# Retention's values and SSD's dt in one pass at the head of the mixers, and S5's products summed on VectorE

## The chip, the cores and the metric

The kernel runs on one core of one Trainium2 chip. The metric is the device time of one execution in microseconds, as the median of several runs; lower is better. The engines are named as the profile names them: PE is TensorE (PEld is its weight load), DVE is VectorE, ACT is ScalarE, POOL is GpSimd, SP is SyncE, which issues all DMA transfers in order.

## What is computed

Two trunk layers of a hybrid backbone run over 640 tokens: a prompt of 128 and a sample of 512, each with its own modulation. All matrices are float32. Cut to what matters:

```python
h = rmsnorm(x, norm1_w) * (1.0 + sc1) + sh1
proj = h @ w_in                                   # 1024 x 2568, split into the four mixers' columns
pa, pb, pc, pd = jnp.split(proj, [o1, o2, o3], axis=-1)
# ssd_mixer:       z, xbc, dt = split(pa);  dt = softplus(dt + dt_bias)  (8 columns: 2 directions x 4 heads)
# retention_mixer: q, k, v, g = split(pb);  y_f, y_b = chunked_decay_scan(q, k, v, ...); silu(g) * groupnorm(y)
# s5_mixer:        bbar = coef * b (complex);  bu = u bbar;  diagonal scan;  y = Re(x c);  GLU
# lru_mixer:       conv, gates, diagonal scan, gelu gate
y = jnp.concatenate([ya, yb, yc, yd], axis=-1) @ w_out
x = x + g1 * y
h = rmsnorm(x, norm2_w) * (1.0 + sc2) + sh2
x = x + g2 * conv_ffn(h, w_up, conv_w, conv_b, w_down)
```

The values are the 256 columns of `v` of the retention mixer, and dt is 8 columns of the SSD mixer.

## The kernel before

Activations stand channels by tokens, as 8 tiles of 128 channels and 640 tokens, in two halves of 320 tokens (`HALF`). A float32 product is made of three float32r matmuls: weight and activation are each split into a rounded part (`hi`) and a remainder (`lo`), and hi*hi, lo*hi and hi*lo are added in PSUM (`mm3`, line 209).

A **column tile** (`col_tile`, 214) is 128 output columns of a weight: 8 k-tiles by 3 matmuls by 2 halves, 48 matmuls of 320 columns. Its weights come through `wsplit` (186): per 512 columns a DMA of 256 KB into a `raw` tile, a cast on ACT into `hi`, a subtraction into `lo`. There are 5 raw tiles (`RAWS`) and 5 pairs of `hi` and `lo` (`SPLITS`), so a tile takes 2 of 5 pairs until its last matmul.

The mixers of a layer are Python generators (`s5_mixer` 820, `lru_mixer` 973, `gates` 1050 for `gb` and `z`, `ssd_mixer` 1110, `ret_mixer` 1277). `layer` (1399) steps them in the order of the string `ORDER` (45). A planner then orders each engine's instructions by a simulated time, with the program's order as priority. Two rules bind it: tiles of one tag in PSUM (`bank`, 139: three `mm`, two `b`, one each of `a`, `c` and `mod`) get their first write in the order of the program (lines 96 to 101), and each engine's queue, SP's too, is worked off in order.

What stands around the change:

- **Layer front.** The half of tokens 320 to 639 is normed first (`HO`). In layer 1 `first_tiles` (232), called at the first step of `s5_mixer`, runs the three first tiles (two of S5, one of LRU) over that half in the banks `mm`, and then over the other half in steps of two k-tiles in `mm`, `a`, `c` and `b`, as the norm delivers them. In layer 0 the norm itself comes in four steps, and `first_tiles` follows them.
- **S5's preparation** (`s5_prep`, 590). For four groups q it makes the products of the input matrix with powers of the state matrix, transposes them into PSUM (`c`), copies them (`wbs`), stores them to DRAM (`wb`) and loads them back for the scans. In layer 1 the complex product is finished on VectorE (`cmul`) and transposed. In layer 0 VectorE makes four real products alone, and the sums are made on PE: `T.matmul` with the identity, two products added in PSUM, and again in the product with `cm`.
- **dt** (1110 to 1137). The 8 columns are the stationary operand, `hi` and `lo` side by side as 16, and `hh` streams: 2 halves by 8 k-tiles by 2 parts, 32 matmuls of 320 columns, then a copy, five transposes and two additions.
- **Values** (1340 to 1359). They stand token-major: the activation is stationary and the weights stream. Five chunks of 128 tokens by 8 k-tiles by 3 matmuls of 256 columns, 120 in all, go to the banks `b`, two chunks in a bank, so their first write comes after that of S5's GLU tiles, which are in `b` too. The four pairs of `hi` and `lo` are all needed until the last chunk. Then comes `attend(0)`.

Of the kernel before, what the change touches and what calls it, by code (L numbers as in the profile page):

```python
# [9 lines left out]
F32 = mybir.dt.float32  # L10
# [33 lines left out]

ORDER = ("s5 gb lru lru gb ssd ssd z lru ssd z ret ret ssd ret ssd ret ret ret ret",
         "s5 ssd gb lru ssd lru gb z lru ssd z ret ssd ret ret ssd ret ret ret ret")
RAWS = 5
# [28 lines left out]
def hybrid_kernel(ctx: ExitStack, tc: tile.TileContext, I, O, dbg=None):  # L76
# [67 lines left out]
    def r2f(ap):  # L144
        return ap.bitcast(F32)
# [40 lines left out]
    def wsplit(ap, n, cut=512, le=None, tag=None):  # L186

        out = []
        for c0 in range(0, n, cut):
            w = min(cut, n - c0)  # L190
            raw = wp.tile([P, 512], F32, tag="raw", name="raw", bufs=RAWS)
            SP.dma_start(raw[:, :w], ap[:, c0:c0 + w])
            if tag:
                hi, lo = page(tag, F32R, "whi")[:, :512], page(tag, F32R, "wlo")[:, :512]
            else:
                hi = wp.tile([P, 512], F32R, tag="hi", name="hi", bufs=SPLITS)
                lo = wp.tile([P, 512], F32R, tag="lo", name="lo", bufs=SPLITS)
# [392 lines left out]
    def s5_prep(l):  # L590
# [94 lines left out]
        for q in range(2):  # L685
# [14 lines left out]
            for h in range(2):  # L700
# [29 lines left out]
             [bb[:, i] for i in range(2)], [bt[:, i] for i in range(2)])  # L730
        if l == 0:
            nbb = paged(p2, [16, 16], "nbb")
            V.tensor_scalar(nbb, bb[:, 1], -1.0, None, op0=M_)
        ncq = paged(p2, [16, 16], "ncq")
# [10 lines left out]
        for q in range(4):  # L745
# [8 lines left out]
            def big(tag):  # L754
                return paged(p3, [4, 8, 16], tag)

            pm, tt = [big("pmr"), big("pmi")], [big("pt1"), big("pt2")]
            if l:
                cmul([wide(bb[:, i]) for i in range(2)], [pwr(v) for v in ap], pm, tt)
                parts = [[v] for v in pm]  # L760

                yield
            else:

                for t, b, a in ((pm[0], bb[:, 0], ap[0]), (tt[0], nbb, ap[1]), (pm[1], bb[:, 1], ap[0]),
                                (tt[1], bb[:, 0], ap[1])):
                    V.tensor_tensor(t, wide(b), pwr(a), op=M_)
                parts = [[pm[0], tt[0]], [pm[1], tt[1]]]
            parts = [[v.rearrange("p k a b -> p k (a b)") for v in vs] for vs in parts]
# [13 lines left out]
            for i in range(2):  # L783
                for j, v in enumerate(parts[i]):
                    for k in range(4):
                        T.matmul(ps[32 * k:32 * k + 32, 0:128], cm[i][:, o + k, :], v[:, k], start=i + j == 0,
                                 stop=i == 1 and j == len(parts[i]) - 1, tile_position=(0, 32 * k))
            kt = paged(p3, [128], "kt")
# [321 lines left out]
    def ssd_mixer(l, hh, y):  # L1110

        dr = smp.tile([P, 8, 8], F32, tag="dtraw", name="dtraw")
        SP.dma_start(dr, I["w_dt"][l].rearrange("p (k c) -> p k c", c=8))
        dw = smp.tile([P, 8, 16], F32R, tag="dtw", name="dtw")
        V.tensor_copy(dw[:, :, 0:8], dr)
        V.tensor_tensor(dw[:, :, 8:16], dr, r2f(dw[:, :, 0:8]), op=S_)
        yield
        if TSC:
            V.tensor_scalar(pr(l, "scw", 0, 20), pr(l, "scw", 0, 20), 0.5, None, op0=M_)
        dtc = page("C", name="dtc")  # L1120
        old = sec[0]
        sec[0] = old + "*"
# [6 lines left out]
        sec[0] = old  # L1129
        ps = bank("c")  # L1130
        for t in range(5):
            T.transpose(ps[:, 16 * t:16 * t + 16], dtc[0:16, 128 * t:128 * t + 128], idn[0:16, 0:16])
        raw = sm([5, 8])
        pv = ps[:, :80].rearrange("p (a b) -> p a b", b=16)
        V.tensor_tensor(raw, pv[:, :, 0:8], pr(l, "dtb").unsqueeze(1).to_broadcast([P, 5, 8]), op=A_)
        V.tensor_tensor(raw, raw, pv[:, :, 8:16], op=A_)
        dt = smp.tile([P, 40], F32, tag="dt", name="dt")
# [137 lines left out]


    def ret_mixer(l, hh, y):
        swap = [(i + 16) % 32 for i in range(32)]
# [60 lines left out]
        yield  # L1339
        units = wsplit(I["w_in"][l, 14], 1024) + wsplit(I["w_in"][l, 15], 1024)  # L1340
        vk = [paged("B", [5, 128], "rv") for _ in range(2)]
        for c0 in (0, 2, 4):
            n = min(2, 5 - c0)
            ps = bank("b")
            old = sec[0]
            sec[0] = old + "*"
            for c in range(n):
                for k in range(8):
                    hi, lo = units[k // 2][2:]
                    w = slice((k % 2) * 256, (k % 2) * 256 + 256)  # L1350

                    mh, ml = [v[:, 128 * (c0 + c):128 * (c0 + c) + 128] for v in hh[k]]
                    o = ps[:, 256 * c:256 * c + 256]
                    T.matmul(o, mh, hi[:, w], start=k == 0, stop=False)
                    T.matmul(o, mh, lo[:, w], start=False, stop=False)
                    T.matmul(o, ml, hi[:, w], start=False, stop=k == 7)
            sec[0] = old
            for i in range(2):
                A.copy(vk[i][:, c0:c0 + n], ps[:, 0:256 * n].rearrange("p (c w) -> p c w", w=256)[:, :, 128 * i:128 * i + 128])
        attend(0, q, kx)  # L1360
# [38 lines left out]
    def layer(l, norm):  # L1399
# [4 lines left out]
        for ks in steps or (range(8),):  # L1404
            if l == 0 and ks[0]:
                mod_first(ks[0] // 2)
            for h in HO:
# [5 lines left out]
                "ret": ret_mixer(l, hh, ys["ret"]), "gb": gates(l, hh, (2, 3), ys["lru"], AF.Gelu_apprx_tanh),  # L1413
                "z": gates(l, hh, (9, 11), ys["ssd"], None if TSZ else AF.Silu)}
        for n in gens:
# [11 lines left out]
        for i, n in enumerate(order):  # L1427
# [364 lines left out]
```

## Time and profile before

| what | value |
|---|---|
| median of 3 runs | 1727.2 us (1725.74 to 1730.68) |
| the profiled execution's own time | 1727.16 us |
| its span, first to last instruction | 1725.4 us |
| PE busy, mean granted clock | 1655.2 us (96%), 0.982 |
| DVE, ACT, POOL busy | 1027.9, 713.1, 230.5 us |
| moved by DMA | 205.99 MB |

The profiled execution is some 1.8 us longer than its span and agrees with the median. Layer 0's mixers lie at about 60 to 390 us of the span, layer 1's at about 928 to 1212 us; the feed-forward parts lie behind each. A busy PE is not a PE at its peak: matmuls overlap, one of 320 columns is shown for 0.31 us, and the next begins 0.15 us after it. All instructions have line 92, the helper that records them, so groups are told apart by their tiles.

### The profile page before, as it was taken

How to read it: one execution, taken by the hardware profiler on the slowest of the kernel's cores; microseconds unless marked ns; L12 is line 12 of the kernel's file. 1: busy time of each engine (PE TensorE's matmuls, PEld its weight loads, DVE VectorE, ACT ScalarE, POOL GpSimd, SP SyncE). 2: the span in 40 equal slices, each digit the busy share in tenths (PEclk: the TensorE clock that was granted, in tenths of full speed). 3: DMA queues.
4: the chain of work that ended last, by engine and by line, in shares of the span. 5: the costliest groups of instructions: out<-in, count | busy, mean ns of one | idle time of the engine just before them, and what ended most of it. 6: DMA issues, size and time to landing. Idle time of an engine off the chain costs nothing.

```text
span 1725.4 us, 31021 instructions
## 1 busy us (share of the span) xinstructions
PE 1655.2 (96%) x11630; PEld 1540.3 (89%) x11630; DVE 1027.9 (60%) x2566; ACT 713.1 (41%) x1567; POOL 230.5 (13%) x445
## 2 busy tenths in 40 slices
PE   7887999999999999999999999999899999999997
PEld 3766887888999999999998998888899999999996
DVE  7776876878783454364357797677754333333346
ACT  5734526645441432232245653663452232232244
POOL 0000001000222111211220010100021211111221
PEclk9989999999999999999999999989999999999999
DMA  9565564321346545554232344422122222322321
GB/s 337 159 186 156 175 190 147 92 77 62 123 143 195 172 151 159 174 173 115 86 117 92 104 134 134 138 66 77 38 68 62 86 75 61 92 74 57 91 74 61
DMA packets 143433, 205.99 MB, mean 119 GB/s; under 512 B 24900, under 2 KB 64692, under 8 KB 143284
## 3 DMA queue, kind: packets, MB, share of 16 engines
q1 hardware_dynamic: 143284, 204.02, 37.7%
q8 instruction: 92, 1.51, 0.4%
q14 instruction: 57, 0.47, 0.1%
HBM read 183.89 MB, written 20.07 MB: 118 GB/s over the span
## 4 chain that ended last, share of the span: by engine, by line
PE 82%; DVE 6%; DMA 3%; ACT 2%; issue 1%; SPq 1%; POOL 0%; DVEq 0%; ACTq 0%
PE mm L92 67%; PE b L92 7%; PE c L92 3%; PE mod L92 3%; PE a L92 2%; DVE x L92 1%; SPq L92 1%; DVE lo L92 1%; DVE nt L92 1%; DMA mraw<-in_mod_w 1%; DMA wb<-wb 0%; DMA scb<-cumd 0%; DVE s5r L92 0%; DVE nsq L92 0%; DVE nacc L92 0%
## 5 line engine op out<-in xcount | busy, mean ns | idle before, releaser
L92 PE MATMUL mm<-hhi,hi 128*128 128x320 f32 x1880 | 594.8, 317 | 7.9 <-ACT hhi L92 5.8
L92 PE MATMUL mm<-hhi,lo 128*128 128x320 f32 x1880 | 590.4, 314 | 3.1 <-DVE lo L92 3.1
L92 PE MATMUL mm<-hlo,hi 128*128 128x320 f32 x1880 | 589.6, 315 | 0.8 <-DVE hlo L92 0.8
L92 ACT CAST hi<-raw 128x512 fp32r<-128x512 f32 (+1 forms) x378 | 223.5, 593 | 512.2 <-PE mm L92 290.6
L92 PEld LDWEIGHTS mm<-hhi,hi 128*128 128x128 f32 x1880 | 357.5, 190 | 25.1 <-issue 7.6
L92 PEld LDWEIGHTS mm<-hhi,lo 128*128 128x128 f32 x1880 | 357.1, 190 | 7.7 <-DVE lo L92 4.6
L92 PEld LDWEIGHTS mm<-hlo,hi 128*128 128x128 f32 x1880 | 356.8, 190 | 6.8 <-DVE hlo L92 1.8
L92 POOL TENSOR_TENSOR lo<-raw,hi 128x512 fp32r<-128x512 f32 (+1 forms) x134 | 166.5, 1243 | 531.0 <-ACT hi L92 324.2
L92 DVE SCALAR_TENSOR_TENSOR x<-mm,mod,x 128x128 f32<-128x128 f32 (+2 forms) x284 | 114.3, 433 | 184.8 <-PE mm L92 183.5
L92 PE MATMUL mm<-fah,lo 128*128 128x320 f32 x640 | 197.4, 309 | 0.0
L92 PE MATMUL mm<-fah,hi 128*128 128x320 f32 x640 | 196.4, 311 | 0.4 <-DVE x L92 0.4
L92 PE MATMUL mm<-fal,hi 128*128 128x320 f32 x640 | 195.9, 309 | 0.0
L92 DVE TENSOR_TENSOR lo<-raw,hi 128x512 fp32r<-128x512 f32 (+1 forms) x244 | 162.7, 668 | 43.9 <-ACT hi L92 39.0
L92 DVE TENSOR_SCALAR fc<-fraw,par 128x643 f32<-128x643 f32 x44 | 27.5, 625 | 189.7 <-ACT fraw L92 189.5
L92 PEld LDWEIGHTS mm<-fah,hi 128*128 128x128 f32 x640 | 119.5, 188 | 4.9 <-issue 1.6
L92 PEld LDWEIGHTS mm<-fah,lo 128*128 128x128 f32 x640 | 120.3, 188 | 0.4 <-issue 0.4
L92 PEld LDWEIGHTS mm<-fal,hi 128*128 128x128 f32 x640 | 119.8, 188 | 0.0
L92 DVE TENSOR_TENSOR fa<-fc,mm 128x320 f32<-128x320 f32 (+1 forms) x128 | 44.1, 374 | 102.8 <-PE mm L92 100.4
L92 DVE SCALAR_TENSOR_TENSOR fc<-fraw,par,fc 128x643 f32<-128x643 f32 x88 | 85.0, 967 | 1.7
L92 ACT COPY fraw<-mm 128x320 f32<-128x320 f32 (+2 forms) x124 | 38.3, 344 | 85.4 <-PE mm L92 82.0
L92 PE MATMUL mod<-mraw,s 128*32 128x256 f32 x768 | 63.5, 395 | 7.7 <-DMA mraw<-in_mod_w 6.8
L92 POOL MEMSET fraw<- 128x2 f32 x132 | 7.4, 101 | 395.4 <-DVE nrs L92 211.5
(395 smaller groups left out, 2518.3 us busy)
## 6 DMA issues: line engine op xcount, KB each, us to landing
raw<-in_up SPq DMA_DIRECT2D x176, 256.0 KB
mraw<-in_mod_w SPq DMA_DIRECT2D x160, 256.0 KB
raw<-in_w_in SPq DMA_DIRECT2D x80, 256.0 KB
raw<-in_dn SPq DMA_DIRECT2D x96, 192.0 KB
mraw<-in_mod SPq DMA_DIRECT2D x32, 256.0 KB
raw<-in_w_o SPq DMA_DIRECT2D x32, 256.0 KB
tb<-tb SPq DMA_DIRECT2D x16, 326.0 KB
x<-in_x SPq DMA_DIRECT2D x16, 320.0 KB
```

Source lines behind the costliest of these rows:

```text
L92: r = f(*a, **k)
```

## The change

A new generator `values` makes the values and dt in one pass. It is first in `ORDER` in both layers. The 8 dt columns of two k-tiles are split into the same tiles as the 256 value columns, so that a k-tile is 264 columns wide, and `SPLITS` tiles grow from 512 to 528 columns. Each chunk of 128 tokens has a bank `mm` of its own and 24 matmuls of 264 columns. dt now comes out token-major and has its bias added straight from PSUM; the 32 matmuls, the copies, the five transposes and the addition of the two parts go away. `ret_mixer` takes the values from `early`. In `s5_prep` layer 0 does what layer 1 does: `cmul` finishes the products on VectorE, and PE transposes and multiplies one tile where it took two. `load_x(0)` and the first call of `filler` move by one place in the order, so they stand behind the same mixer step as before.

```diff
-ORDER = ("s5 gb lru lru gb ssd ssd z lru ssd z ret ret ssd ret ssd ret ret ret ret",
-         "s5 ssd gb lru ssd lru gb z lru ssd z ret ssd ret ret ssd ret ret ret ret")
+ORDER = ("v s5 gb lru lru gb ssd ssd z lru ssd z ret ret ssd ret ssd ret ret ret ret",
+         "v s5 ssd gb lru ssd lru gb z lru ssd z ret ssd ret ret ssd ret ret ret ret")
...
             pm, tt = [big("pmr"), big("pmi")], [big("pt1"), big("pt2")]
+            cmul([wide(bb[:, i]) for i in range(2)], [pwr(v) for v in ap], pm, tt)
             if l:
-                cmul([wide(bb[:, i]) for i in range(2)], [pwr(v) for v in ap], pm, tt)
-                parts = [[v] for v in pm]
                 yield
-            else:
-                for t, b, a in ((pm[0], bb[:, 0], ap[0]), (tt[0], nbb, ap[1]), (pm[1], bb[:, 1], ap[0]),
-                                (tt[1], bb[:, 0], ap[1])):
-                    V.tensor_tensor(t, wide(b), pwr(a), op=M_)
-                parts = [[pm[0], tt[0]], [pm[1], tt[1]]]
...
                 for k in range(4):
-                    for j, v in enumerate(parts[i]):
-                        if l:
-                            T.transpose(ps[:, 128 * k:128 * k + 128], v[:, k], idn)
-                        else:
-                            T.matmul(ps[:, 128 * k:128 * k + 128], v[:, k], idn, start=j == 0, stop=j == 1)
+                    T.transpose(ps[:, 128 * k:128 * k + 128], pm[i][:, k], idn)
...
     def ssd_mixer(l, hh, y):
-        dr = smp.tile([P, 8, 8], F32, tag="dtraw", name="dtraw")
-        SP.dma_start(dr, I["w_dt"][l].rearrange("p (k c) -> p k c", c=8))
-        dw = smp.tile([P, 8, 16], F32R, tag="dtw", name="dtw")
-        V.tensor_copy(dw[:, :, 0:8], dr)
-        V.tensor_tensor(dw[:, :, 8:16], dr, r2f(dw[:, :, 0:8]), op=S_)
...
-        for o, n in HALF:
-            ps = bank("mm")
-            for k in range(8):
-                for j in range(2):
-                    T.matmul(ps[:16, :n], dw[:, k], hh[k][j][:, o:o + n], start=k + j == 0, stop=k + j == 8)
-            A.copy(dtc[0:16, o:o + n], ps[:16, :n])
...
+    def values(l, hh):
+        dr = smp.tile([P, 8, 8], F32, tag="dtraw", name="dtraw")
+        SP.dma_start(dr, I["w_dt"][l].rearrange("p (k c) -> p k c", c=8))
+        yield
+        vk = early["vk"] = [paged("B", [5, 128], "rv") for _ in range(2)]
+        raw = early["dt"] = smp.tile([P, 5, 8], F32, tag="dtsum", name="dtsum")
+        units = []
+        for j in range(4):
+            wr = wp.tile([P, 512], F32, tag="raw", name="raw", bufs=RAWS)
+            SP.dma_start(wr, I["w_in"][l, 14 + j // 2][:, 512 * (j % 2):512 * (j % 2) + 512])
+            hi = wp.tile([P, 528], F32R, tag="hi", name="hi", bufs=SPLITS).rearrange("p (k c) -> p k c", c=264)
+            lo = wp.tile([P, 528], F32R, tag="lo", name="lo", bufs=SPLITS).rearrange("p (k c) -> p k c", c=264)
+            for v, c in ((wr.rearrange("p (k c) -> p k c", c=256), slice(0, 256)), (dr[:, 2 * j:2 * j + 2], slice(256, 264))):
+                A.copy(hi[:, :, c], v)
+                V.tensor_tensor(lo[:, :, c], v, r2f(hi[:, :, c]), op=S_)
+            units += [(hi[:, k], lo[:, k]) for k in range(2)]
+        for c in range(5):
+            ps = bank("mm")
...
+            for k in range(8):
+                hi, lo = units[k]
+                mh, ml = [v[:, 128 * c:128 * c + 128] for v in hh[k]]
+                T.matmul(ps[:, 0:264], mh, hi, start=k == 0, stop=False)
+                T.matmul(ps[:, 0:264], mh, lo, start=False, stop=False)
+                T.matmul(ps[:, 0:264], ml, hi, start=False, stop=k == 7)
...
+            for i in range(2):
+                A.copy(vk[i][:, c], ps[:, 128 * i:128 * i + 128])
+            V.tensor_tensor(raw[:, c], ps[:, 256:264], pr(l, "dtb"), op=A_)
...
     def ret_mixer(l, hh, y):
...
-        units = wsplit(I["w_in"][l, 14], 1024) + wsplit(I["w_in"][l, 15], 1024)
-        vk = [paged("B", [5, 128], "rv") for _ in range(2)]
-        for c0 in (0, 2, 4):
-            n = min(2, 5 - c0)
-            ps = bank("b")
...
+        vk = early["vk"]
         attend(0, q, kx)
...
-            if i == 0 and l == 0:
+            if i == 1 and l == 0:
                 load_x(0)
-            if l == 0 and i >= 1:
+            if l == 0 and i >= 2:
                 filler(FPS)
```

## Rows read from the trace of the kernel before

**Rows 1.** The page: busy time of the engines; the chain that ended last.

```profile
PE 1655.2 (96%) x11630; PEld 1540.3 (89%) x11630; DVE 1027.9 (60%) x2566; ACT 713.1 (41%) x1567; POOL 230.5 (13%) x445
PE 82%; DVE 6%; DMA 3%; ACT 2%; issue 1%; SPq 1%; POOL 0%; DVEq 0%; ACTq 0%
```

**Rows 2.** Busy time by stretch, layer 0: length, PE, PEld, DVE, ACT, POOL, clock, DMA.

```profile
83.00:105.00 22.00, 11.21 (x98) 8.69 (x99) 11.20 (x24) 9.07 (x24) 1.39 (x8) 0.82 0.65 207
...
256.00:277.00 21.00, 16.96 (x111) 12.00 (x108) 13.33 (x46) 12.96 (x35) 3.04 (x3) 0.92 0.61 200
277.00:294.00 17.00, 17.00 (x142) 16.24 (x141) 10.33 (x26) 9.36 (x24) 2.69 (x7) 1.00 0.24 82
```

**Rows 3.** The same view for stretches of layer 1.

```profile
928.00:943.00 15.00, 12.87 (x81) 11.78 (x80) 12.04 (x30) 6.45 (x17) 0.00 (x0) 1.00 0.44 138
...
958.00:1060.00 102.00, 101.69 (x697) 96.77 (x695) 89.44 (x214) 57.91 (x114) 11.32 (x51) 1.00 0.42 133
...
1081.00:1094.00 13.00, 10.74 (x51) 6.70 (x50) 8.63 (x28) 9.03 (x26) 3.06 (x3) 1.00 0.18 57
1094.00:1110.00 16.00, 16.00 (x137) 15.38 (x136) 10.84 (x25) 9.19 (x23) 3.15 (x8) 1.00 0.52 182
```

**Rows 4.** The chain of waits, pieces in order of time: start, length, what.

```profile
447.81 28.68 PE mm L92 x192
...
1103.26 6.95 PE b L92 x59
```

**Rows 5.** dt's tiles: duration in ns, least, median and most; first and last start.

```profile
L92 PE MATMUL mm<-hhi,dtw x32: 303/306/501, 127.0 to 957.4; 128*16 128x320 f32 x32
L92 DVE TENSOR_TENSOR dtw<-dtraw,dtw x2: 215/220/225, 34.7 to 154.3; 128x64 fp32r<-128x64 f32 x2
...
L92 PE MATMUL c<-ct,dtc x10: 207/208/231, 154.0 to 962.6; 16*128 16x16 f32 x10
```

**Rows 6.** Timeline of PE, S5's first group in layer 0: start, length, what, wait.

```profile
88.92 0.80 PE L92 MATMUL c<-ct,pmr 128*128 128x128 f32 x2 [5.26 <-DVE pmr L92]
...
95.17 0.39 PE L92 MATMUL c<-ct,pt 128*128 128x128 f32 x2
95.39 0.39 PE L92 MATMUL c<-ct,pmi 128*128 128x128 f32 x2
...
97.20 0.43 PE L92 MATMUL c<-pmi,cm 128*32 128x128 f32 x8
...
103.28 1.64 PE L92 MATMUL b<-s5u,wb 128*128 128x81 f32 x8 [3.32 <-DMA wb<-wb]
```

**Rows 7.** S5's product tile, its sum on VectorE (layer 1's preparation among them).

```profile
L92 DVE TENSOR_TENSOR pmr<-pmr,pt x12: 680/684/1783, 98.7 to 796.0; 128x512 f32<-128x512 f32 x12
```

**Rows 8.** Timeline of PE, layer 1's preparation: four transposes of a finished product.

```profile
642.69 0.60 PE L92 MATMUL c<-ct,pmi 128*128 128x128 f32 x4
```

**Rows 9.** Timeline of SP's queue in layer 0: successive loads of column-tile weights.

```profile
256.00 0.33 SPq L92 DMA_DIRECT2D raw<-in_w_in  x1
...
292.14 2.04 SPq L92 DMA_DIRECT2D raw<-in_w_in  x2
```

**Rows 10.** The same in layer 1.

```profile
1078.59 0.33 SPq L92 DMA_DIRECT2D raw<-in_w_in  x1
...
1109.51 1.04 SPq L92 DMA_DIRECT2D raw<-in_w_in  x2
```

**Rows 11.** Timeline of PE at the front of layer 1.

```profile
927.89 0.31 PE L92 MATMUL mm<-fal,hi 128*128 128x320 f32 x1
928.04 0.31 PE L92 MATMUL mm<-hhi,hi 128*128 128x320 f32 x1
...
942.46 0.41 PE L92 MATMUL a<-hhi,hi 128*128 128x320 f32 x1 [1.65 <-ACT hhi L92]
```

**Rows 12.** Timeline of PE at layer 1's second norm, after a longer wait.

```profile
1250.72 0.63 PE L92 MATMUL a<-hhi,hi 128*128 128x320 f32 x1 [2.96 <-ACT hhi L92]
1251.15 0.47 PE L92 MATMUL a<-hhi,lo 128*128 128x320 f32 x1
1251.42 0.47 PE L92 MATMUL c<-hhi,hi 128*128 128x320 f32 x1
...
1253.82 0.39 PE L92 MATMUL c<-hlo,hi 128*128 128x320 f32 x1
```

More of the change, by code (lines that the diff above doesn't have):

```diff
@@ L195, in wsplit @@
             else:
-                hi = wp.tile([P, 512], F32R, tag="hi", name="hi", bufs=SPLITS)
-                lo = wp.tile([P, 512], F32R, tag="lo", name="lo", bufs=SPLITS)
+                hi = wp.tile([P, 528], F32R, tag="hi", name="hi", bufs=SPLITS)
+                lo = wp.tile([P, 528], F32R, tag="lo", name="lo", bufs=SPLITS)
             A.copy(hi[:, :w], raw[:, :w])
@@ L730, in s5_prep @@
              [bb[:, i] for i in range(2)], [bt[:, i] for i in range(2)])
-        if l == 0:
-            nbb = paged(p2, [16, 16], "nbb")
-            V.tensor_scalar(nbb, bb[:, 1], -1.0, None, op0=M_)
         ncq = paged(p2, [16, 16], "ncq")
@@ L757, in s5_prep @@
             pm, tt = [big("pmr"), big("pmi")], [big("pt1"), big("pt2")]
+            cmul([wide(bb[:, i]) for i in range(2)], [pwr(v) for v in ap], pm, tt)
             if l:
-                cmul([wide(bb[:, i]) for i in range(2)], [pwr(v) for v in ap], pm, tt)
-                parts = [[v] for v in pm]
                 yield
-            else:
-                for t, b, a in ((pm[0], bb[:, 0], ap[0]), (tt[0], nbb, ap[1]), (pm[1], bb[:, 1], ap[0]),
-                                (tt[1], bb[:, 0], ap[1])):
-                    V.tensor_tensor(t, wide(b), pwr(a), op=M_)
-                parts = [[pm[0], tt[0]], [pm[1], tt[1]]]
-            parts = [[v.rearrange("p k a b -> p k (a b)") for v in vs] for vs in parts]
+            pm = [v.rearrange("p k a b -> p k (a b)") for v in pm]
             for i in range(2):
@@ L783, in s5_prep @@
             for i in range(2):
[L784 to L787, printed above, removed]
+                for k in range(4):
+                    T.matmul(ps[32 * k:32 * k + 32, 0:128], cm[i][:, o + k, :], pm[i][:, k], start=i == 0, stop=i == 1,
+                             tile_position=(0, 32 * k))
             kt = paged(p3, [128], "kt")
@@ L1120, in ssd_mixer @@
         dtc = page("C", name="dtc")
-        old = sec[0]
-        sec[0] = old + "*"
-        for o, n in HALF:
-            ps = bank("mm")
-            for k in range(8):
-                for j in range(2):
-                    T.matmul(ps[:16, :n], dw[:, k], hh[k][j][:, o:o + n], start=k + j == 0, stop=k + j == 8)
-            A.copy(dtc[0:16, o:o + n], ps[:16, :n])
[L1129 to L1136, printed above, removed]
+        raw = early["dt"]
         dt = smp.tile([P, 40], F32, tag="dt", name="dt")
@@ L1274, in ssd_mixer @@
                 V.scalar_tensor_tensor(yy, yy, nw[:, t:t + 1], rs, op0=M_, op1=M_)
+    early = {}
+    def values(l, hh):
[16 more added lines that the diff above has]
+            ps = bank("mm")
+            old = sec[0]
+            sec[0] = old + "*"
+            for k in range(8):
[4 more added lines that the diff above has]
+                T.matmul(ps[:, 0:264], ml, hi, start=False, stop=k == 7)
+            sec[0] = old
+            for i in range(2):
+                A.copy(vk[i][:, c], ps[:, 128 * i:128 * i + 128])
+            V.tensor_tensor(raw[:, c], ps[:, 256:264], pr(l, "dtb"), op=A_)
     def ret_mixer(l, hh, y):
@@ L1339, in ret_mixer @@
         yield
-        units = wsplit(I["w_in"][l, 14], 1024) + wsplit(I["w_in"][l, 15], 1024)
-        vk = [paged("B", [5, 128], "rv") for _ in range(2)]
-        for c0 in (0, 2, 4):
-            n = min(2, 5 - c0)
-            ps = bank("b")
[L1345 to L1359, printed above, removed]
+        vk = early["vk"]
         attend(0, q, kx)
@@ L1413, in layer @@
                 "ret": ret_mixer(l, hh, ys["ret"]), "gb": gates(l, hh, (2, 3), ys["lru"], AF.Gelu_apprx_tanh),
-                "z": gates(l, hh, (9, 11), ys["ssd"], None if TSZ else AF.Silu)}
+                "v": values(l, hh), "z": gates(l, hh, (9, 11), ys["ssd"], None if TSZ else AF.Silu)}
         for n in gens:
```

## The prediction, made before the changed kernel was built

> **What bounds the kernel now.** I read the page first: PE is busy for 96% of the span and holds 82% of the chain that ended last [rows 1]. So PE's time is the first candidate. Busy time flatters it, though, because matmuls overlap. The chain of waits gives the true pitch: 192 matmuls of 320 columns in 28.68 us are 0.149 us each, and 59 matmuls of 256 columns in 6.95 us are 0.118 us [rows 4]. Then I read busy time by stretch, looking for stretches in which PE issues less than it could.
>
> There are three kinds. In layer 0 from 83 to 105 us PE is busy for 11.21 of 22 us at a granted clock of 0.82 [rows 2]; the timeline shows it waiting for S5's first products (5.26 us) and, at 103.28, for their way through DRAM (3.32 us) [rows 6]. Next, from 256 to 277 us PE starts 111 instructions in 21 us, and from 277 to 294, when it runs the values, 142 in 17 us, or 0.120 us each [rows 2]. At that rate 111 take 13.3 us, so 7.7 us are lost. Layer 1 has the same pair: 51 in 13 us, then 137 in 16 us, 0.117 each [rows 3]; 51 take 6.0 us, so 7.0 are lost. SP's queue says why no column tile fills the hole. Weights are loaded at 256.00 and not again until 292.14, and at 1078.59 and not again until 1109.51 [rows 9, 10]: the values' four weight pairs are held while their matmuls wait, by the order of the banks `b`, behind S5's GLU, and one pair of five is left for the stream. Last, the front of layer 1: the last matmul of the layer before starts at 927.89, the first one on the new layer's early half follows at 928.04, and the late half arrives only at 942.46 [rows 11].
>
> **The change part by part.** I work against the profiled execution's 1727.16 us, which is the median of the runs (1727.2) for this purpose.
>
> *dt, both layers.* Removed per layer: 32 matmuls of 320 columns [rows 5] by 0.149 = 4.8 us, and five transposes by some 0.1 us, 0.5 us (they show 0.208 with overlap [rows 5]). Added: 8 columns on 120 matmuls. The two pitches give (0.149 - 0.118) / 64 us a column, so 120 x 8 columns cost 0.5 us; if 264 columns cost as much as 320, it is 3.7 us. I take 0.5, since 264 lies next to 256. All of it is on PE, the bound: -4.8 us a layer, -9.6 us in all (bounds -6.4 and -9.6). The small casts and additions on ACT and DVE are of the size of one 0.220 us row [rows 5], some eight more a layer than now; they lie under PE's work, and if that cover were gone they would cost 1.8 us a layer. I take nothing.
>
> *S5's products, layer 0.* Per group q PE now does 32 passes for the two transposed sums, 0.22 us per two at full clock [rows 6], so 3.5 us, and 32 of 0.027 (0.22 us per eight, four such rows a group [rows 6]), 0.9 us. Afterwards it is two sets of four transposes by 0.60 us [rows 8] and half of the 0.9: 1.65 us. PE saves 2.75 us a group, 11.0 in four. DVE adds two sums of 0.684 us [rows 7] a group, 5.5 us, less a small negation. For the chain to the scans, one set is now 16 passes, 1.76 us at full clock; then it is 0.68 + 0.60 = 1.28. That is -0.5 a set, -1 a group; for the first group, which runs at the low clock (4.3 us for its first set, from 88.92 [rows 6] to the filler after it), I estimate -3. Bounds for the part: -11 (all PE time counts) and +5.5 (DVE's time counts and PE's doesn't). I take -5: PE is not the bound in 83 to 105 [rows 2], and the chain's -3 and two of the later groups' gains remain.
>
> *The values move, layer 0.* 120 matmuls, 14.6 us with their new width, leave 277 to 294 and go ahead of `gb`, as do four loads of 256 KB and dt's on SP's queue. Early they displace other column tiles by the same 14.6 us; that is zero in itself (bound: -10, if they fill the idle half of 83 to 105 [rows 2]). What is gained is the hole: with the pairs free, the tiles of the later mixers stream on through 256 to 277, -7.7 at most. What is late next is SSD's own chain there, which shares DVE (13.33 of 21 us busy [rows 2]). I take -7 (bounds 0 and -10).
>
> *The values move, layer 1.* Now they come ahead of S5's first tiles. Their first chunk is tokens 0 to 127, in the half that is normed last, and they use the banks `mm`, whose first writes keep the program's order. So no first tile can start before the values' chunks have begun, and the 72 matmuls of the early half (3 tiles x 8 x 3), 72 x 0.149 = 10.7 us, that fill the time from 928.04 to 942.46 [rows 11], have nothing to stand in for them. Queued behind the values' first matmul on PE is everything else of the layer; S5's, LRU's and the GELU gate's work on ACT and DVE waits for it. I take +10.7 (bounds 0, if the norm came that much earlier, and +14.4, the whole stretch of rows 11). PE then begins after a long idle time: at the second norm, after 2.96 us of waiting, ten matmuls run at 0.27 us until 1253.82 [rows 12], which cost 10 x 0.12 = 1.2 us; after only 1.65 us at 942.46 the granted clock stays at 1.00 [rows 11, 3]. So +1.2. Against it stands the hole of 7.0 us, of which I take -6 (bounds 0 and -7). S5's and LRU's first tiles end later, by the values' 14.6 us plus the idle 10.7 less dt's 4.8, 20 us. DVE was busy for 89.44 of 102 us in the stretch after [rows 3], so it can catch up 12.6 us, and the 16 us that the values held between GLU and `attend(0)` [rows 3] absorb the rest. I take 0 (bound +8).
>
> The Trainium skill, "TensorE: Matmul & The Clock Gate", section "HAM oscillation — how this bites in real kernels", speaks against this front: an array left waiting falls to its half rate, so the work that follows starts cold and the wait is paid for twice. Rows 12 agree. Without that rule the sum would be 1.2 us lower.
>
> *Sum.* -9.6 - 5 - 7 + 10.7 + 1.2 - 6 = -15.7; I round DVE's fuller schedule up to +1.5 and take -14: **1713 us**.
>
> **The rivals.**
>
> *Slower: layer 1's front is not paid back.* The 20 us by which S5 and LRU begin later don't vanish in DVE's slack; its 12% of slack is spread between waits and not to be had, so GLU ends 17 us or more later than 1094. For: DVE is at 88% there [rows 3]. Against: the 16 us of the values are gone from the tail. Price: front 10.7 + 1.2, plus 20 late less 4 of the freed tail, less dt's 4.8 there, +23 in layer 1; layer 0 keeps -13 (its -16.8 with SSD's chain taking half of the hole). +10: 1737 us. It decides from a GLU end past 1110 us on the old time scale.
>
> *No change: the gains lie in waits.* dt's first half and S5's products lie in stretches where PE waits anyway, the holes are bound by SSD's chain and not by missing tiles, and layer 1's front eats the rest. For: the chain in the holes passes through ACT and DVE. Sum: -5 - 3 - 6 + 10.7 + 1.2 = -2: 1725 us.
>
> *The front costs nothing, or it isn't what runs first.* The planner might not hold the tiles back (an order that I read in the program, not in a trace), or the values fill the idle half of 83 to 105. Then +11.9 is gone or -10 comes on top: about 1701 us.
>
> **How the numbers follow.** Forecast (1706 to 1721) 0.48; slower 0.16; no change 0.17; better than 1706 0.19, about a third of it below 1697. About 0.3%, 5.2 us, is what a measurement of this kernel can tell from no change. Faster: 0.48 + 0.19 = 0.67. Same: 0.17. Slower: 0.16. The range 1697 to 1735 leaves out 0.06 below and some 0.12 above, and takes in the terms' bounds except when several fall on the same side.
>
> **What would show it.** Right: no dt matmuls and no `c<-ct,pt` products; weight loads that go on through the former holes at 256 to 292 and 1079 to 1109; GLU followed at once by `attend(0)`'s matmuls; in layer 1 a PE gap of some 10 us before the values with half-rate matmuls behind it; S5's first tiles there about 20 us later. The prediction is wrong if layer 1's early half still runs ahead of the values, if the weight loads stop all the same, if 264 columns have a pitch well above 0.122 us, or if DVE in layer 0's preparation becomes what the scans wait for.

## The result, and the profile after

| | before | after |
|---|---|---|
| median, same chip, 4 runs each | 1727.0 us (1725.7 to 1730.7) | 1715.3 us (1715.0 to 1715.8) |
| ratio to before, 95% interval | | 0.993 [0.9918, 0.9943] |
| the profiled execution's own time, its span | 1727.16, 1725.4 us | 1715.24, 1713.4 us |
| mean granted clock | 0.982 | 0.974 |

11.7 us less; the forecast was 14 less. The number was right. Most of the reason was not, and the first sign of it is a split by stage. The borders below are starts of PE instructions in each trace: the last `b<-rsq,ct` (the group norm's sum, near the end of a layer's mixers) and the last matmul `mm<-fal,hi` of the down product, the second product of the feed-forward part.

| stretch | before | after | difference | forecast |
|---|---|---|---|---|
| layer 0, start to last `b<-rsq,ct` | 384.7 | 374.9 | -9.8 | -16.8 (dt, S5, values) |
| from there to layer 0's last down matmul | 543.2 | 541.4 | -1.8 | 0 |
| layer 1, from there to last `b<-rsq,ct` | 279.4 | 285.9 | +6.5 | +1.1 (dt, front, cold clock, hole) |
| from there to layer 1's last down matmul | 504.8 | 497.4 | -7.4 | 0 |
| sum | | | -12.4 | -14 with the rounding |

9 of the 12 us lie in the output product and the feed-forward parts, which the change does not edit. The mixers, which carry every term of the forecast, gave 3.3.

The page of after: busy time, then the chain that ended last (for [rows 1]).

```profile
PE 1633.3 (95%) x11396; PEld 1514.5 (88%) x11396; DVE 1031.7 (60%) x2583; ACT 714.3 (42%) x1581; POOL 233.0 (14%) x445
PE 82%; DVE 8%; DMA 4%; ACT 3%; issue 2%; SPq 1%; DVEq 0%; POOL 0%; ACTq 0%; POOLq 0%
```

PE is busy 21.9 us less, more than the time that was gained. Busy time by stretch in layer 0 of after (for [rows 2]; length, PE, PEld, DVE, ACT, POOL, clock, DMA):

```profile
83.00:105.00 22.00, 20.49 (x155) 17.70 (x153) 18.12 (x55) 14.74 (x39) 1.26 (x8) 1.00 0.77 238
105.00:180.00 75.00, 56.48 (x370) 43.87 (x370) 55.45 (x110) 28.92 (x60) 5.22 (x25) 0.80 0.62 183
256.00:277.00 21.00, 15.00 (x102) 11.16 (x101) 16.73 (x60) 12.44 (x36) 0.73 (x1) 0.76 0.38 119
277.00:294.00 17.00, 16.33 (x93) 12.90 (x92) 13.12 (x28) 9.70 (x25) 6.65 (x11) 1.00 0.60 185
```

The second of these stretches in before:

```profile
105.00:180.00 75.00, 66.36 (x518) 54.63 (x518) 51.42 (x101) 30.28 (x59) 5.08 (x25) 0.92 0.54 160
```

There are two holes to see. The idle half of 83 to 105 is filled (11.21 busy of 22 us became 20.49, clock 0.82 became 1.00). But 105 to 180, which had 518 instructions at 0.92, now has 370 at 0.80: the hole moved and grew. And 256 to 277 is not filled: 102 instructions at a clock of 0.76, against 111 at 0.92; 277 to 294, where the values ran (142 instructions), now holds 93. SP's queue in after (for [rows 9]) says why:

```profile
243.86 0.33 SPq L92 DMA_DIRECT2D raw<-in_w_in  x1
248.49 0.32 SPq L92 DMA_DIRECT2D raw<-in_w_o  x1
253.59 0.38 SPq L92 DMA_DIRECT2D raw<-in_w_o  x1
288.14 0.33 SPq L92 DMA_DIRECT2D raw<-in_w_o  x1
```

At 243.86 the layer's last weights of `w_in` are loaded; what follows belongs to the output product, which needs the mixers' results. No tile is held back any more. There is none left to run.

Layer 1 of after, by stretch (for [rows 3]), and PE's timeline at its front (for [rows 11]):

```profile
916.30:930.00 13.70, 2.81 (x7) 1.22 (x5) 11.97 (x30) 5.63 (x12) 0.00 (x0) 0.66 0.52 168
930.00:950.00 20.00, 19.93 (x143) 19.93 (x144) 10.18 (x32) 11.29 (x35) 0.61 (x6) 0.89 0.00 1
950.00:1060.00 110.00, 108.22 (x737) 104.32 (x736) 85.83 (x192) 61.74 (x119) 11.06 (x41) 1.00 0.38 117
1060.00:1097.00 37.00, 32.34 (x229) 30.22 (x228) 25.88 (x75) 13.27 (x35) 2.41 (x11) 0.83 0.45 129
1097.00:1113.00 16.00, 15.03 (x62) 8.96 (x59) 11.69 (x37) 11.95 (x35) 3.52 (x7) 0.86 0.43 148
```

```profile
916.30 0.31 PE L92 MATMUL mm<-fal,hi 128*128 128x320 f32 x1
924.55 1.44 PE L92 MATMUL mod<-nacc,ct 128*128 128x320 f32 x2 [7.94 <-DVE nacc L92]
925.78 1.27 PE L92 MATMUL mod<-nsq,ct 128*128 128x320 f32 x2
930.07 0.59 PE L92 MATMUL mm<-hi,hhi 128*128 128x264 f32 x1 [3.02 <-ACT hhi L92]
930.45 0.42 PE L92 MATMUL mm<-lo,hhi 128*128 128x264 f32 x1
930.67 0.42 PE L92 MATMUL mm<-hi,hhi 128*128 128x264 f32 x1
```

This is the forecast's front, wait by wait: nothing stands in for the early half, PE waits 7.94 and 3.02 us, and the values begin at 0.22 us each, half rate, where the same kind later starts every 0.120 to 0.125 us. Layer 1's hole isn't filled either: 1060 to 1113 has 291 instructions in 53 us. SP's queue (for [rows 10]) shows the same as in layer 0, loads of `w_in` that run out:

```profile
1067.45 3.78 SPq L92 DMA_DIRECT2D raw<-in_w_in  x2
1077.11 0.32 SPq L92 DMA_DIRECT2D raw<-in_w_o  x1
```

### The profile page after: what moved, and what is told of

It reads as the page before. It is cut to its first block, busy times and chain, and to the rows that moved or that the text cites. A ratio compares the mean times of both kernels' runs of the same rounds, so it can differ in the third digit from the quotient of the medians.

```text
span 1713.4 us, 30635 instructions
## 1 busy us (share of the span) xinstructions
PE 1633.3 (95%) x11396; PEld 1514.5 (88%) x11396; DVE 1031.7 (60%) x2583; ACT 714.3 (42%) x1581; POOL 233.0 (14%) x445
## 4 chain that ended last, share of the span: by engine, by line
PE 82%; DVE 8%; DMA 4%; ACT 3%; issue 2%; SPq 1%; DVEq 0%; POOL 0%; ACTq 0%; POOLq 0%
PE mm L92 67%; PE b L92 6%; PE mod L92 4%; PE c L92 2%; PE a L92 2%; SPq L92 1%; DMA mraw<-in_mod_w 1%; DVE x L92 1%; DVE nt L92 1%; DMA scb<-cumd 1%; DVE lo L92 1%; DVE hlo L92 1%; DVE nsq L92 1%; DVE nacc L92 0%; DVE s5r L92 0%
## 5 line engine op out<-in xcount | busy, mean ns | idle before, releaser
L92 PE MATMUL mod<-mraw,s 128*32 128x256 f32 x768 | 68.4, 400 | 13.5 <-DMA mraw<-in_mod_w 12.1
```

The lines of the kernel that those rows point to most:

```text
L92: r = f(*a, **k)
```

## The experiments

All medians in one table, each with its ratio to before on the same chip (before was 1725.2 to 1727.0). `Half rate` is time in us, read from one profile's granted clock: over stretches of 5 us, (1 - clock) x 2 x length, summed over the mixers of layer 0 (from 20 us on) and of layer 1. An edit to the work lets the planner order the instructions anew, at times in the layer that the edit leaves alone too; the kernels that move places alone (pad_only, shift, lo_gap, after_same_place, and pad_s5 against s5_only) keep the order of PE.

| kernel | median us | ratio, 95% interval | half rate, layer 0 + layer 1 |
|---|---|---|---|
| before | 1727.0 | | 34 + 14 |
| after | 1715.3 | 0.993 [0.9918, 0.9943] | 48 + 31 |
| pad_only | 1714.5 | 0.993 [0.9909, 0.9951] | 31 + 3 |
| s5_only | 1721.4 | 0.997 [0.9952, 0.9989] | 55 + 14 |
| v_only | 1717.2 | 0.9945 [0.9925, 0.9964] | 31 + 31 |
| l1_s5_first | 1748.7 | 1.0126 [1.0111, 1.0142] | 51 + 51 |
| l0_only | 1716.6 | 0.9947 [0.993, 0.9963] | 55 + 14 |
| l1_only | 1729.7 | 1.0015 [1.0003, 1.0027] | 55 + 34 |
| l1_rev | 1715.2 | 0.994 [0.9925, 0.9955] | 41 + 27 |
| old_dt | 1719.6 | 0.9963 [0.9948, 0.9978] | 41 + 17 |
| pad_s5 | 1712.8 | 0.9925 [0.9905, 0.9944] | 51 + 14 |
| shift | 1726.3 | 0.9995 [0.9985, 1.0005] | 45 + 14 |
| lo_gap | 1716.2 | 0.9941 [0.9923, 0.9959] | 34 + 17 |
| after_same_place | 1717.2 | 0.9955 [0.9939, 0.9971] | 51 + 31 |

**The width of the tiles alone** (pad_only: the kernel before with 16 unused columns).

```diff
-                hi = wp.tile([P, 512], F32R, tag="hi", name="hi", bufs=SPLITS)
-                lo = wp.tile([P, 512], F32R, tag="lo", name="lo", bufs=SPLITS)
+                hi = wp.tile([P, 528], F32R, tag="hi", name="hi", bufs=SPLITS)
+                lo = wp.tile([P, 528], F32R, tag="lo", name="lo", bufs=SPLITS)
```

> The kernel before with one edit: the tiles hi and lo are 528 columns wide instead of 512 (no instruction reads the 16 new columns; only the tiles' places in SBUF move). Theory A, the terms of the prediction: nothing in the sum belongs to this, so 1727 us within 1.5, and the pitch of the feed-forward matmuls stays as before. Theory B, placement: in the trace of before every twelfth matmul of an up tile starts 153 to 165 ns after the last instead of 145, and in the trace of after no such place is left in layer 1; if the new places alone do this, this kernel has the faster pitch (mean below 147 ns in both up stages, no period of twelve) and gains the 4 to 6 us that layer 1's feed-forward part gained, perhaps 2 more in the mixers and layer 0: 1718 to 1723 us.

Measured: 1714.5, 12 us less, as much as the whole change. The instructions stand in the same order on every engine as in before; only places in SBUF differ. Theory B named the direction and too small a size. One row of the chain of waits shows it best, the piece of 2818 matmuls that runs from layer 1's second norm to its end; what differs in it is the **pitch**, the time from one matmul's start to the next. Before:

```profile
803.44 100.46 PE mm L92 x681
1271.22 416.73 PE mm L92 x2818
```

After:

```profile
792.34 99.89 PE mm L92 x681
1264.25 411.42 PE mm L92 x2818
```

pad_only:

```profile
1263.32 412.32 PE mm L92 x2818
```

The chain leaves PE nowhere in these pieces, and they hold the same matmuls. The 4 to 5 us in the longer one are pitch alone. Another 4 to 5 us of pad_only's profile are no pitch: in before PE falls to half rate around attention in layer 1, and in pad_only it doesn't. That it comes of the new places isn't shown: lo_gap below, which has the shorter pitch too, has as much half rate in layer 1 as before has (17 us against 14). Two stretches in before:

```profile
1125.90:1130.90 5.00, 4.17 (x22) 2.77 (x23) 4.35 (x14) 4.65 (x15) 0.00 (x0) 0.68 0.17 45
1130.90:1135.90 5.00, 5.00 (x24) 3.34 (x23) 1.71 (x5) 0.91 (x3) 0.53 (x1) 0.50 0.00 0
```

The same two in pad_only, 2 us earlier:

```profile
1123.90:1128.90 5.00, 4.21 (x33) 2.82 (x35) 4.38 (x14) 4.62 (x15) 0.00 (x0) 1.00 0.15 48
1128.90:1133.90 5.00, 5.00 (x37) 4.54 (x36) 4.29 (x13) 2.41 (x6) 0.53 (x1) 1.00 0.16 52
```

**What about the place matters** (shift, lo_gap). In before hi and lo of a pair both begin at byte 736 of a 2048-byte grid, since every tile is 2048 bytes a partition. shift moves all of them by 512 bytes:

```diff
+    gap = wp.tile([P, 128], F32, tag="gap", name="gap", bufs=1)
+    nc.vector.memset(gap, 0.0)
```

> The kernel before with one edit: a tile of 128 columns (512 bytes a partition) is laid ahead of raw, hi and lo, so that these ten tiles and the small ones behind them move by 512 bytes and keep their distance of 2048. In before all ten tiles of hi and lo begin at byte 736 of a 2048-byte grid, and the late starts are those of the matmuls whose weights are in the second 128 columns of a tile. Theory A, a certain place on the grid is slow: now the first 128 columns lie there, and the late starts move to the first k-tile of each four; time as before, 1727 within 3. Theory B, the distance between the tiles is what counts: the late starts stay with the second k-tile; 1727 within 3. Theory C, the place of the weights against the place of the activations: the late starts go away or become fewer; 1714 to 1724.

lo_gap moves only the five tiles `lo`, by 64 bytes:

```diff
+                if not gap:
+                    gap.append(wp.tile([P, 16], F32, tag="gap", name="gap", bufs=1))
+                    nc.vector.memset(gap[0], 0.0)
                 lo = wp.tile([P, 512], F32R, tag="lo", name="lo", bufs=SPLITS)
```

> The kernel before with one edit: 64 bytes are laid between the five tiles hi and the five tiles lo, so that raw and hi stay where they are, every tile keeps 2048 bytes to the next of its kind, and only lo moves by 64 bytes against hi. Theory A, hi and lo at the same place of the grid is what is slow: the period of twelve (146 146 154 159 164 150 144 146 144 142 142 143 ns) is gone, both up stages run at 146.5 ns or less on the mean, 3 to 8 us less than before, 1718 to 1723. Theory B, the distance from one buffer of hi to the next is what counts: the period stays, 148.3 ns in layer 1, time as before within 2 us.

Measured: shift 1726.3, no change; lo_gap 1716.2, 9 to 10 us less, 2 us under theory A's range. Both keep PE's order. The chain's two pieces in shift:

```profile
806.44 100.46 PE mm L92 x681
1273.93 416.74 PE mm L92 x2818
```

and in lo_gap:

```profile
798.53 99.42 PE mm L92 x681
1266.19 411.12 PE mm L92 x2818
```

What is late can be read from PE's timeline in an up tile, a column tile of the feed-forward part's first product (start, length). A **unit** is what one pair of `hi` and `lo` serves in one half of the tokens: four k-tiles by three matmuls. Before, from a unit's first matmul on:

```profile
1400.65 0.31 PE L92 MATMUL mm<-hhi,hi 128*128 128x320 f32 x1
1400.80 0.31 PE L92 MATMUL mm<-hhi,lo 128*128 128x320 f32 x1
1400.95 0.32 PE L92 MATMUL mm<-hlo,hi 128*128 128x320 f32 x1
1401.10 0.33 PE L92 MATMUL mm<-hhi,hi 128*128 128x320 f32 x1
1401.26 0.33 PE L92 MATMUL mm<-hhi,lo 128*128 128x320 f32 x1
1401.42 0.31 PE L92 MATMUL mm<-hlo,hi 128*128 128x320 f32 x1
1401.57 0.31 PE L92 MATMUL mm<-hhi,hi 128*128 128x320 f32 x1
```

lo_gap:

```profile
1400.10 0.31 PE L92 MATMUL mm<-hlo,hi 128*128 128x320 f32 x1
1400.24 0.31 PE L92 MATMUL mm<-hhi,hi 128*128 128x320 f32 x1
1400.39 0.30 PE L92 MATMUL mm<-hhi,lo 128*128 128x320 f32 x1
1400.53 0.31 PE L92 MATMUL mm<-hlo,hi 128*128 128x320 f32 x1
```

In ns, the steps in before and in shift are 146 146 154, 159 164 150, 144 146 144, 142 142 143 for the four k-tiles of a unit, and then the same again; in lo_gap's units there they lie between 141 and 148. Of the last 1536 up matmuls of layer 1, 375 step by 153 ns or more in before and in shift, none in lo_gap and none in after; the mean is 148.27, 148.27, 145.04 and 145.64 ns. So theory B of shift holds as far as this goes: the late starts stay with the second k-tile, and a move of all by 512 bytes, the length of a k-tile, doesn't count; a smaller one wasn't tried. And theory A of lo_gap holds: 64 bytes between hi and lo end the late starts. Whether it is the distance of the two or the new place of `lo` that ends them, lo_gap alone can't tell.

**The change without its placement** (after_same_place: after with 1728 bytes laid between the tiles `hi` and `lo`).

```diff
+            gap.append(wp.tile([P, 432], F32, tag="gap", name="gap", bufs=1))
...
-        rows = smp.tile([P, 512], F32, tag="modtt", name="modtt")[:, 0:256]
+        rows = smp.tile([P, 256], F32, tag="modtt", name="modtt")
```

> The kernel after, its instructions in the same order on every engine, with 1728 bytes laid between the five tiles hi and the five tiles lo (a small tile that used half of its columns is halved to make room), so that each lo lies 12288 bytes, six times 2048, behind its hi: hi and lo of a pair are at the same place of the grid again, as in the kernel before; the buffers still begin 2112 bytes apart. Theory A, all that after gained over before comes with the places and the moved work is worth about nothing: 9 to 12 us more than after, 1724 to 1728, with late starts again in the up tiles (mean of both up stages 147.5 ns or more). Theory B, the moved work carries the gain: within 3 us of after, 1712 to 1718, whatever the pitch does. Between them, 1719 to 1723: half and half, or the distance between buffers matters too.

Measured: 1717.2, ratio 0.9955 [0.9939, 0.9971] against after's 0.993: the median lies in theory B's range. The late starts came back only in part, though, which the chain shows:

```profile
1267.64 413.64 PE mm L92 x2818
```

150 of 1536 steps are late, the three of a unit together in 47 of 128 units, and the mean is 146.61 ns. They are in two of five buffers, and in PE's timeline of the up tiles one of them is late in its second k-tile, the next but one in its fourth. By the addresses in the program these are the first and the third pair, at bytes 736 and 864 of the grid; the other three, the last at 992 among them, have no late starts of this kind, though hi and lo are at the same place there too. So the same place for hi and lo is not enough by itself, and this kernel doesn't undo the placement as fully as I meant; it can't say how much of after's gain the moved work carries.

**S5's sums alone** (s5_only: these lines and their counterparts in the transposes on the kernel before) **and left out** (v_only: after with them undone).

```diff
+            cmul([wide(bb[:, i]) for i in range(2)], [pwr(v) for v in ap], pm, tt)
-                for t, b, a in ((pm[0], bb[:, 0], ap[0]), (tt[0], nbb, ap[1]), (pm[1], bb[:, 1], ap[0]),
-                                (tt[1], bb[:, 0], ap[1])):
-                    V.tensor_tensor(t, wide(b), pwr(a), op=M_)
```

> The kernel before with S5's part alone: layer 0's products are summed on VectorE, values and dt stay as they were. Theory A, the forecast's term: -5 us (bounds -11 and +5.5), so about 1722, with the first S5 scan some 3 us earlier than 103.3. Rival: PE's time saved lies in stretches where PE waits, and DVE's two sums a group stand in the chain instead: 1727 within 1.5, the first scan not earlier.

> The kernel after with S5's part undone: values and dt first in both layers and 528 columns, but layer 0's products summed on PE as before. Theory A: 1715.3 + 5 = 1720. Rival: S5's part is worth nothing here or costs, since the first scan came 9 us later after the change: 1713 to 1716, and if the sums on VectorE are what delayed the scan, it starts earlier than 112.5 again; if it still starts at about 112, the values ahead of it delay it.

Measured: s5_only 1721.4, -5 [-8, -2], the forecast's size. Its chain was wrong, though. PE's timeline in s5_only (for [rows 6]):

```profile
92.65 1.12 PE L92 MATMUL c<-ct,pmr 128*128 128x128 f32 x4
94.44 1.12 PE L92 MATMUL c<-ct,pmi 128*128 128x128 f32 x4 [0.68 <-ACT wbs L92]
105.44 0.81 PE L92 MATMUL b<-s5u,wb 128*128 128x81 f32 x5
```

The first transposes start 3.7 us later than in before and the first scan 2.2 later, not 3 earlier; the later groups pay (the last transpose of a product at 142.3 against 146.5, GLU's last matmul at 273.1 against 277.3). In v_only the first scan starts at 107.0, against 112.5 in after: of the 9 us that after is late there, VectorE's sums make over half. All the same v_only is 1.9 us slower than after, within the scatter.

**dt as before** (old_dt).

```diff
-                T.matmul(ps[:, 0:264], mh, hi, start=k == 0, stop=False)
+                T.matmul(ps[:, 0:256], mh, hi[:, 0:256], start=k == 0, stop=False)
...
-        raw = early["dt"]
+        for o, n in HALF:
+            ps = bank("mm")
+            for k in range(8):
+                for j in range(2):
+                    T.matmul(ps[:16, :n], dw[:, k], hh[k][j][:, o:o + n], start=k + j == 0, stop=k + j == 8)
...
```

> The kernel after with dt as before: values first with 256 columns in tiles of the same 528, dt by its own 32 matmuls of 320 columns, copies, transposes and addition in SSD's first step. Theory A, the forecast's dt term (-4.8 us a layer, all on the bound): 9.6 us more than after, 1725. Rival: dt's matmuls lie in stretches where PE waits anyway: some 0 to 3 us more than after, 1715 to 1718, most of it in layer 1, where PE is busiest in that place.

Measured: 1719.6, 4 us more than after (6 by the ratios). Layer 0's last down matmul starts at 916.1 against 916.3: there dt's matmuls cost nothing. From there to layer 1's last one it is 786.4 us against 783.4. So dt is worth about half of the forecast, and what the profile shows of it, 3 us, lies in layer 1.

**Layer 1's front** (l1_rev, l1_s5_first).

```diff
-        for c in range(5):
+        for c in (3, 4, 2, 1, 0) if l else range(5):
```

> The kernel after with one edit: layer 1's five chunks of values run in the order 3, 4, 2, 1, 0, so that the two chunks that lie wholly in the half normed first can run while the late half is on its way. Theory A, the wait at the front is what costs: 48 matmuls at 0.122 us, 5.9 us, move into the 11 us before 930, the array is less cold when the rest begins, and S5's and LRU's first tiles come as much earlier: 5 to 8 us less than after, 1707 to 1710. Rival: the costly thing in layer 1 is that S5's and SSD's chains begin late and that the holes before retention stay empty, and 6 us at the front are absorbed there: within 2 us of after, 1713 to 1717, though the values end 5 us or more earlier.

```diff
-         "v s5 ssd gb lru ssd lru gb z lru ssd z ret ssd ret ret ssd ret ret ret ret")
+         "s5 v ssd gb lru ssd lru gb z lru ssd z ret ssd ret ret ssd ret ret ret ret")
```

> The kernel after with one edit: in layer 1 the values come second, behind S5's first step, so that the three first tiles run over the early half again while the norm's late half is on its way. Theory A, the front's price as forecast: the 11 to 14 us in which PE waited and ran at half rate from 916.3 to 934 are filled with 72 matmuls, 8 to 12 us less than after: 1703 to 1707. Rival: what is won at the front is lost in the waits for S5's and SSD's chains before the end of the mixers: within 2 us of after, 1713 to 1717, with the second norm's restart not earlier than in after.

Measured: l1_rev 1715.2, the same as after. The early chunks do run in the gap:

```profile
917.00:930.70 13.70, 10.28 (x55) 9.07 (x53) 10.70 (x26) 5.71 (x13) 0.00 (x0) 0.75 0.48 169
```

55 instructions instead of 7, the values end 3.5 us earlier counted from the last layer's end, GLU 2.8 earlier, and nothing of it reaches the end of the mixers. l1_s5_first lost 33 us and turned out to be no test of the front. The front is filled, but behind it comes a new wait. Two stretches, then ACT's timeline:

```profile
916.30:930.00 13.70, 12.30 (x78) 11.23 (x76) 10.75 (x26) 5.20 (x14) 0.00 (x0) 1.00 0.45 149
951.00:1021.00 70.00, 50.77 (x222) 42.72 (x221) 50.53 (x131) 19.25 (x47) 8.21 (x37) 0.63 0.44 130
```

```profile
1019.68 0.44 ACT L92 ACTIVATE glut<-b 128x320 f32<-128x320 f32 x1 [1.76 <-PE b L92]
1020.01 1.11 ACT L92 COPY rv<-mm 128x128 f32<-128x128 f32 x6
```

The values' first three chunks were done by 951.1 and stood in the three banks `mm`, and ACT, working in its order, copied them out only at 1020.01, behind S5's whole chain. For 70 us no column tile has a bank (222 instructions, clock 0.63), and dt, now tied to the values, reaches SSD's cumulative sum at 1045 instead of 974.

**By layer** (l0_only, l1_only: after with the other layer's values and dt as before; pad_s5: s5_only with 528 columns, in the same order as s5_only). l0_only, and l1_only with the condition reversed and layer 0's order restored:

```diff
-         "v s5 ssd gb lru ssd lru gb z lru ssd z ret ssd ret ret ssd ret ret ret ret")
+         "s5 ssd gb lru ssd lru gb z lru ssd z ret ssd ret ret ssd ret ret ret ret")
...
-        vk = early["vk"]
+        if l:
+            units = wsplit(I["w_in"][l, 14], 1024) + wsplit(I["w_in"][l, 15], 1024)
...
```

> The kernel after with layer 1 as it was: there the values stand behind retention's second rotation, in the banks b, and dt has its own 32 matmuls; order of layer 1 as before. Layer 0 keeps the change, S5's sums stay on VectorE, tiles stay 528 wide. Theory A, the move to the head of layer 1 costs net: from the last matmul of layer 0's feed-forward part to the first of layer 1's down product (the row mm<-fa) before takes 400.2 us, the kernel with 528 columns alone 393.5, after 403.9; with layer 1 restored it is 393 to 395 again, and the whole is 9 to 11 us below after: 1704 to 1707. Theory B, the forecast's terms for layer 1 (-4.8 + 10.7 + 1.2 - 6 = +1): the same as after within 2 us, 1713 to 1717.

> The kernel after with layer 0's values and dt as before; layer 1 keeps values and dt first, S5's sums and 528 columns stay. With the kernel that moves them in layer 0 alone (1716.6), this gives the move's price by layer. Forecast's terms: layer 1's move +1, layer 0's -12, so against after this one is 12 us slower, 1727. Rival: layer 0's move is worth 0 to -6, since after is at half rate for 48 us there against 34 before: 1715 to 1721.

> S5's sums on VectorE and tiles of 528 columns, nothing else: values and dt in both layers as in the kernel before. The order of the instructions on every engine is that of the kernel with S5's part alone, so the two differ by the places in SBUF only. Theory A, the parts add up: -12 for the places and -5 for S5, 1708 to 1711 us, so that moving values and dt (after: 1715.3) costs some 5 us net. Rival: the gains overlap, since part of the 12 us is half-rate time that comes and goes with the waits in the mixers: 1713 to 1717, and moving values and dt is worth nothing either way.

Measured: neither layer moved 1712.8, layer 0 alone 1716.6, layer 1 alone 1729.7, both 1715.3. l0_only and l1_only came out near what the forecast's terms say (1713 to 1717 and 1727), but pad_s5 did not: moving both costs 2 to 3 us against moving none, inside the scatter, and does not gain the 11 us that the terms for dt, values and front promise. Places and S5 come 3 us short of adding up (1712.8, not 1709.5), within the interval; pad_s5 is 9 us faster than s5_only in the same order. By layer the medians make no sense as a sum, and I leave that open. Two things disturb it. The pitch is not the same in all four: the late starts of the up tiles are back in l0_only and l1_only (84 and 78 of the last 1536, where after has none and pad_s5 13), with tiles of the same width. The chain's piece in l0_only, then in l1_only:

```profile
1267.39 413.67 PE mm L92 x2818
```

```profile
1272.04 413.60 PE mm L92 x2818
```

And layer 0 of l0_only is ordered otherwise than that of after, and later. One profile each says this much, counted to the second norm's first matmul `mod<-nacc,ct`, since in l0_only, v_only and old_dt that matmul follows the last `b<-rsq,ct` of one layer 4 to 6 us later than in after: layer 1's mixers, from the last down matmul on, take 297.9 and 297.2 us in pad_s5 and l0_only, 303.6 in after and 307.5 in l1_only, so the move costs 6 to 10 there; layer 0 gets that far at 395.8 and 399.8 without the move (l1_only and pad_s5, PE's order in layer 0 the same, so 4 us are scatter), and at 392.5 in after and 399.9 in l0_only with it. pad_s5 and after can't be told apart; no kernel here is surely faster than after.

## Why the number was right and the working was not

*Pitch.* I took 0.149 us [rows 4] as a constant of a 320-column matmul. It holds late starts that the placement makes, and the change's 528 columns removed them. The placement, at zero in my sum, is worth 9 to 12 us by itself on the kernel before (lo_gap, pad_only; in pad_only's profile some 5 of them are a half-rate stretch less, not pitch), and with 9 us gained in stages that the change doesn't touch it is most of the result. The edit stood in the diff; I costed its columns and not its addresses.

*264 columns.* 0.120 to 0.125 us, as estimated.

*dt, -9.6.* Failing step: "all of it is on PE, the bound". In layer 0 it was nothing, in all 4 to 6. The bounds (-6.4 and -9.6) were both drawn from PE's time, and neither asked whether PE was waiting there, though [rows 2] gave the clock of 0.82 nearby. The first of them was miscounted besides: 4.8 + 0.5 - 3.7 is 1.6 us a layer, -3.2 in all.

*S5, -5.* Right by s5_only, with a wrong path: the first group became later. What I named as a sign of failure, VectorE holding up the scans in layer 0, did happen in part: the first scan starts at 112.5 against 103.3, and 5.5 of these 9.2 us go when the sums are undone (v_only, 107.0).

*Values, layer 0, -7.* The hole at 256 to 277 wasn't filled, since the column tiles' loads ran out at 244. The weight loads stop all the same, another of my signs of failure, though no pairs are held. PE's longest waits there are for the scans (2.5 us, VectorE's `s5r`) and for SSD's own chain (2.2 us, `sE`), and the scans are late: GLU's last matmul starts at 289.7 against 277.3. What I held at zero, the idle half of 83 to 105, was filled, and lost again at 105 to 180. The layer's mixers gave 9.8 instead of 16.8.

*Values, layer 1.* The wait, its causes and the half-rate start came as written, and S5's first scan starts 23 us later, counted from the last layer's end (62.7 against 40.1), near the 20 forecast for its first tiles. The -6 for the hole did not come: the hole from 1060 to 1113 is longer than the old one. The price of the front as a term of the sum was wrong all the same: giving half of it back (l1_rev) moved nothing, so it wasn't what ended last. GLU's last matmul starts 196.1 us after the last layer's end instead of 164.7, 31 later, past the point from which I let the slower rival decide, and the tail behind it, to the last `b<-rsq,ct`, is 25 us shorter (89.8 against 114.7). That rival's mechanism took place, but the tail gave back 25, where its price allowed 4. What remains is the +6.5 of the table, against +1.1.

*The clock.* I charged one cold start, 1.2 us. The mixers of after stand at half rate for 31 us more than those of before (48 + 31 against 34 + 14). Layer 0's part seems to go with S5's sums and not with the values: kernels with the sums on VectorE have 41 to 55 us there, before's order has 31 to 45, and v_only 31. Layer 1's part goes with the values: 27 us or more wherever they come first or second, old_dt with 17 excepted, against 3 to 17 elsewhere. Work taken from PE where PE waits anyway would make its waits longer, and the clock fall with them. I take this for the place where much of the work saved on PE went; it is argued from these sums, and no run isolates it. Half rate alone doesn't set the time either: s5_only has 21 us more of it than before and is 5 us faster.

So the number was luck: the range and the direction held because two errors of some 10 us cancelled. The mixers gave 11 less than forecast, the addresses 9 that weren't in it.

## What to carry to other kernels

An edit that changes the size of a tile moves everything behind it: before crediting a gain to the work that moved, compare the pitch in stages that the edit doesn't touch, and time a twin with the new addresses and the old order. Split the result by stage against each term, also when the total fits. And time taken from PE counts only where PE was the last to be waited for, as dt's did in layer 1 and not in layer 0.

## What the runs showed of the hardware

The pitch of a float32r matmul depends on where its weights lie: with hi and lo of a pair at the same byte of the 2048-byte grid, three starts in twelve come 8 to 18 ns late (148.27 ns on the mean, 145.04 with 64 bytes between them), the same within 1 ns in 125 of the last 128 units of layer 1's up tiles in before. A common move by 512 bytes changes nothing. In after_same_place only two buffers of five show it, each in another k-tile, and in l0_only and l1_only some starts of 153 to 157 ns are back with tiles of after's width, so more than the distance of hi and lo counts: the activations' places, or the order in which the buffers follow each other. Neither was tried by itself. The Trainium skill, "SBUF — State Buffer", section "SBUF: two separate sides", knows contention only on the port that GpSimd and VectorE share and on the DMA side. The same matmuls in the same order got faster here by a move of `lo` alone, so the measurement decides: TensorE's operands have places that cost. Whether they cost by contention no run shows.

A single execution's time scatters by some 5 us to either side, and it goes with the clock: of before's 17 runs beside pad_s5, the slowest, 1731.15 us, had a mean clock of 0.979, and the fastest, 1721.54, one of 0.985. One fall to half rate more or less, as the one at attention above, is 4 to 5 us.
